# An encoder on one core: tiles moved within a partition, no instruction moved

## The chip, the cores and the metric

The kernel runs on one core of a Trainium2 chip. The metric is the device time of one execution in microseconds. Before the change it is 599.91 us, the median of three runs (599.82 to 600.35).

## What is computed

Two layers, each a mixer and a feed-forward, on 256 tokens of 1,024 numbers, all in float32:

```
for l in range(2):
    h = rms_norm(x, norm1_g[l]);  proj = h @ w_in[l]            # 1024 x 2560
    out_a, out_d, out_c = three kinds of attention on parts of proj (4, 6 and 6 heads of 64)
    mix = concat(rms_norm(out_a), rms_norm(out_d), rms_norm(out_c)) * out_norm_g[l]
    x = x + mix @ w_out[l]                                      # 1024 x 1024
    h = rms_norm(x, norm2_g[l])
    g, u = split(h @ w_gate_up[l], 2)                           # 1024 x 5632
    g = depthwise_conv_of_3(g, conv_w[l]) + conv_b[l]
    x = x + (gelu(g) * u) @ w_down[l]                           # 2816 x 1024
```

## The kernel before

**Products in parts.** A float32 matrix is split into a high part `hi`, rounded to the format `float32r` that TensorE takes, and a low part `lo`, the rest. A product is then a sum of matmuls of parts. Weights come in units of up to 2,048 columns per partition: a DMA on SP's queue brings a unit to a tile `wp_raw` (4 of them), ScalarE casts it to `wp_hi`, VectorE subtracts to get `wp_lo` (2 tiles of each), in pieces of 512 or 1,024 columns (`split`, line 716). Activations are split in the same way: `act_hT` holds the turned, normed input of a layer's half, high and low part side by side (512 numbers for each of 8 blocks of 128 features); `act_mixT_hi` and `act_mixT_lo` the turned attention output; `act_ch` and `act_cl` the gated activations of the feed-forward.

**Kinds of matmul.** A matmul takes 128 columns of one operand as its stationary weights and streams the other operand past them. The names in a row of the profile stand as out<-stream and weights, not always in that order, so here is which is which:

- *Projections* (`mm3` in `projections`, line 942): three matmuls per block, `act_hT` stationary, `wp_hi` or `wp_lo` streamed, 384, 256 or 512 columns wide, into the accumulators `psa_a`.
- *Output projection* (line 966): the same, with `act_mixT_*` stationary, 512 wide. For a few of its units in the second layer, weights that were split earlier are kept in other tiles (`act_qc`, `act_kc`, `act_mixT_*`).
- *Gate and up* (`half_up`, line 1369): the weights are stationary. For each of 8 blocks `large` streams 512 columns of `act_hT` (high and low part) past `wp_hi`, and `little` streams 256 (the high part) past `wp_lo`, into `psw_w`. Mostly eight large ones follow each other, then eight little ones.
- *Down* (`down`, line 1456): `act_ch` or `act_cl` stationary, `wp_hi` or `wp_lo` streamed, 512 wide, into `psa_a`. The last block of columns at the very end is done in halves of 256.

Transposes, scores and the products of probabilities with values are smaller matmuls of other tiles.

**Order.** The kernel records all its operations and then orders them with a planner of its own: costs by engine and shape, and a table `PLACES` that shifts single operations. Every instruction is issued from line 511, so all rows of the profile have that line. The steps of the feed-forward follow the list `FFN` (line 82): gate, down of the step before, up.

**Places in memory.** Each partition's tiles lie one behind the other, in the order in which they are first used. `Slots.place` (line 180) makes a tile as wide as its widest user; the allocator rounds its size up to 32 bytes. So one small tile early on moves all that come after it. In the program before, counted in bytes from the start of a partition, modulo 256:

```
tile                                       before   after the change
act_hT (weights, or the stream)                96       0
wp_hi                                          96       0
wp_lo, projections, output and down            96       0
wp_lo, gate and up                             96     224
act_mixT_hi, act_mixT_lo                      224       0
act_ch, act_cl                                 64       0
act_qc, act_kc, act_qo, act_ko, act_pT, act_z 224       0
const_ident                                   128       0
const_x                                       128       0
const_v (values)                               64       0
```

Inside these tiles the operands of full products begin at multiples of 512 bytes, so the numbers above are those of the operands too.

Of the kernel before, what the change touches and what calls it, by code (L numbers as in the profile page):

```python
# [12 lines left out]
F32R = mybir.dt.float32r  # L13
# [5 lines left out]
P = 128  # L19
S = 256  # L20
NT = S // P
D = 1024
# [14 lines left out]
UNIT = 2048  # L37
BANK = 512
NS2K = 5
NPT = 9  # L40

TURN_ACT = ("d", "dca")
# [4 lines left out]
RAWS, PARTS, AHEAD, CHUNK = 4, 2, 2, 512  # L47
# [34 lines left out]
FFN = [("G", 0), ("U", 0)]  # L82
# [88 lines left out]
class Slots:  # L171
# [7 lines left out]

    def place(self, t):  # L180
        if t.slot not in self.places:
            shape = list(t.shape) if self.dram else [P, BANK if self.psum else self.cols]
            self.places[t.slot] = self.pool.real.tile(
                shape, self.dtype, tag=f"{self.tag}{t.slot}", name=f"{self.pool.name}_{self.tag}{t.slot}", bufs=1
            )
        return self.places[t.slot]
# [83 lines left out]
class Plan:  # L270
# [5 lines left out]
    def pool(self, real, name, bufs, space=bass.MemoryType.SB):  # L276
        return PlanPool(self, real, name, bufs, space)
# [76 lines left out]
    def order(self):  # L354
# [82 lines left out]
        while len(done) < len(ops):  # L437
# [27 lines left out]
            for t in o.tiles:  # L465
                if t.slot is None:
                    s = t.pool
                    s.given += 1
                    place = min(s.free)
                    s.free.remove(place)  # L470
                    t.since, t.slot = taken_at(place[0], ""), place[1]
# [89 lines left out]
def encoder_kernel(  # L561
# [25 lines left out]
    const = pool("const", 1)  # L587
    wp = pool("wp", 3)
    act = pool("act", 2)
    small = pool("small", 4)  # L590
# [12 lines left out]

    gl0 = act.tile([16, P], F32, tag="s2k", name="gl0", bufs=NS2K)
    gl1 = act.tile([32, P], F32, tag="s2k", name="gl1", bufs=NS2K)
    gains = const.tile([P, 3, DEPTH, KD], F32, tag="gains", name="gains")
# [10 lines left out]
        nc.vector.tensor_copy(gains[:, i : i + n].rearrange("p a l k -> p (a l k)"), ps[:, :w])  # L617


    warm = const.tile([P, P], mybir.dt.bfloat16, tag="warm", name="warm")  # L620
    nc.gpsimd.memset(warm, 1.0)
    nc.gpsimd.memset(ident, 0.0)
    nc.gpsimd.affine_select(ident, ident, [[-1, P]], ALU.not_equal, 1.0, base=0, channel_multiplier=1)
# [42 lines left out]
    PER_LAYER = len(views) // DEPTH  # L666
    LAST_OUT = PER_LAYER - len(FFN)
# [48 lines left out]
    def split(i):  # L716
        v = views[i]
        a, b = v.shape[1], v.shape[2]
        n = a * b
        raw = raws[i]  # L720
        if isinstance(raw, list):
            parts.append(raw)
            return
        hi = wp.tile([P, UNIT], F32R, tag="hi", name=f"hi{i}", bufs=PARTS)
        lo = wp.tile([P, UNIT], F32R, tag="lo", name=f"lo{i}", bufs=PARTS)
        h = b if i < 2 else b * max(1, CHUNK // b)
        if i in kept:
            for d, z in zip(kept[i], (hi, lo)):
                nc.gpsimd.dma_start(z[:, :n], d)
        for c in range(0, n if i not in kept else 0, h):  # L730
            e = min(c + h, n)
            nc.scalar.copy(hi[:, c:e], raw[:, c:e])
            nc.vector.tensor_tensor(lo[:, c:e], raw[:, c:e], hi[:, c:e].bitcast(F32), op=ALU.subtract)
        r = lambda z: z[:, :n].rearrange("p (a b) -> p a b", b=b)
        parts.append((r(hi), r(lo)))

    def unit():

        i = taken[0]
        taken[0] += 1  # L740
        with nc.later(SPLIT_LATER):
            while len(raws) < min(i + AHEAD + RAWS - PARTS, len(views)):
                load(len(raws))
            while len(parts) < min(i + AHEAD, len(views)):
                split(len(parts))
        return parts[i]
# [40 lines left out]
    def mean_squares(name):  # L787

        ss = small.tile([P, NT, 2], F32, tag="ssx", name=f"ssx_{name}", bufs=2)
        for h in range(2):  # L790
            for t in range(NT):
                junk = act.tile([P, 512], F32, tag="s2k", name=f"sq_{name}{t}{h}", bufs=NS2K)
                nc.scalar.activation(
# [136 lines left out]
    for l in range(DEPTH):  # L930
# [3 lines left out]
        if l == 0:  # L934
            gains_T(0, 1)
            split(0)
# [78 lines left out]
        def normed(ps, nh, t, name):  # L1015

            w = nh * HD
            sq = act.tile([P, 512], F32, tag="s2k", name=f"sq_{name}", bufs=NS2K)
            ss = small.tile([P, 8], F32, tag="ss", name=f"ss_{name}")
# [80 lines left out]
        class Head:  # L1100
# [4 lines left out]
            def softens(self, sps, whole):  # L1105

                name, bias = self.name, self.bias
                self.p = p = act.tile([P, NT, S], F32, tag="s2k", name=f"p_{name}", bufs=NS2K)
                nm = small.tile([P, NT], F32, tag="nm", name=f"nm_{name}")
                rs = small.tile([P, NT], F32, tag="rs", name=f"rs_{name}")  # L1110

                if bias is not None:
                    sb = act.tile([P, NT, S], F32, tag="s2k", name=f"sb_{name}", bufs=NS2K)
                    for t in range(NT):
# [22 lines left out]
            def turn(self):  # L1137
# [7 lines left out]
                odd = self.h % 2  # L1145
                self.pT = act.tile([P, NT, S], F32, tag="pT", name=f"pT_{name}", bufs=NPT)
                with nc.later(TURN_LATER):
# [436 lines left out]
```

## Time and profile before

| | |
|---|---|
| median of three runs | 599.91 us |
| the profiled execution | 599.53 us |
| its span, first to last instruction | 597.4 us |
| TensorE, busy | 592.0 us, 3,424 matmuls |
| VectorE, busy | 471.0 us |
| ScalarE, busy | 412.7 us |
| GpSimd, busy | 77.1 us |
| granted TensorE clock | 1.000 |
| moved by DMA | 121.37 MB |

How to read the rows: PE is TensorE, PEld its weight load, DVE VectorE, ACT ScalarE, POOL GpSimd. In the list of groups a row has the line, the engine, the operation, the tiles as out<-in without their numbers, the shape and how often it occurs, then the busy time in us, the mean of one in ns, and the engine's idle time before them. In the timeline a row has its start and length in us and how many like instructions follow each other in it (x8). A stretch (`200.00:270.00`) has its length, the busy time and count of PE, PEld, DVE, ACT and POOL, then the granted clock, the DMA engines' busy share and GB/s. A matmul's busy time overlaps with the next one's, since they are pipelined: the distance between starts is what a matmul takes from the span.

### The profile page before, as it was taken

The numbers are of one execution on the slowest core, as the hardware profiler recorded it, in microseconds if no ns is written. First come the engines' busy times: TensorE is split into PE (matmuls) and PEld (weight loads), VectorE is DVE, ScalarE is ACT, GpSimd is POOL, SyncE is SP. The second block draws the span as 40 slices with busy tenths as digits, with TensorE's granted clock in tenths as the row PEclk, the third lists the DMA queues.
The fourth block names the chain that finished last, engine by engine and source line by source line (L and its number), as shares of the span: only waits on it lengthen the run. The fifth ranks groups of instructions, "written<-read, shape, count | busy, mean of one in ns | idle before, by whom it ended". The sixth has DMA issues, their size and how long they took to land.

```text
span 597.4 us, 9676 instructions
## 1 busy us (share of the span) xinstructions
PE 592.0 (99%) x3424; PEld 509.8 (85%) x3424; DVE 471.0 (79%) x983; ACT 412.7 (69%) x1035; POOL 77.1 (13%) x126
## 2 busy tenths in 40 slices
PE   8999999999999999999999999999999999999997
PEld 6999787888888888888899988778888888888886
DVE  5789889878778998698866897768886777668865
ACT  7789987785574677577686998676756656556661
POOL 1723211250000000000032314311000000000000
PEclk9999999999999999999999999999999999999999
DMA  8995315465599699899455727942554664665701
GB/s 281 300 273 163 110 36 159 164 211 189 185 257 360 223 344 306 295 315 332 157 159 156 251 71 247 356 157 90 188 169 161 202 202 137 212 211 183 234 7 71
DMA packets 85072, 121.37 MB, mean 203 GB/s; under 512 B 9864, under 2 KB 69736, under 8 KB 85024
## 3 DMA queue, kind: packets, MB, share of 16 engines
q1 hardware_dynamic: 82752, 112.10, 57.5%
q0 software_dynamic: 1728, 8.39, 4.0%
q8 instruction: 27, 0.44, 0.3%
q10 hardware_dynamic: 544, 0.26, 0.1%
q14 instruction: 21, 0.17, 0.1%
HBM read 110.86 MB, written 9.88 MB: 202 GB/s over the span
## 4 chain that ended last, share of the span: by engine, by line
PE 97%; ACT 1%; DMA 1%; SPq 0%; issue 0%; DVE 0%; ACTq 0%
PE psw_w L511 51%; PE psa_a L511 46%; DMA const_x<-in_x_dram 1%; ACT act_s2k L511 0%; ACT act_hT L511 0%; ACT wp_hi L511 0%; SPq L511 0%; DVE const_x L511 0%; ACTq L511 0%
## 5 line engine op out<-in xcount | busy, mean ns | idle before, releaser
L511 DVE TENSOR_TENSOR wp_lo<-wp_raw,wp_hi 128x512 fp32r<-128x512 f32 (+2 forms) x332 | 234.4, 736 | 42.3 <-ACT wp_hi L511 31.0
L511 ACT CAST wp_hi<-wp_raw 128x512 fp32r<-128x512 f32 (+2 forms) x332 | 203.7, 668 | 22.1 <-PE psa_a L511 11.0
L511 PE MATMUL psw_w<-act_hT,wp_hi 128*128 128x512 f32 x704 | 182.2, 393 | 0.0
L511 PEld LDWEIGHTS psw_w<-act_hT,wp_hi 128*128 128x128 f32 x704 | 128.2, 189 | 23.7
L511 PE MATMUL psa_a<-wp_hi,act_hT 128*128 128x384 f32 (+2 forms) x448 | 112.0, 333 | 0.3 <-ACT wp_hi L511 0.3
L511 PEld LDWEIGHTS psw_w<-act_hT,wp_lo 128*128 128x128 f32 x704 | 99.1, 190 | 7.4
L511 PE MATMUL psw_w<-act_hT,wp_lo 128*128 128x256 f32 x704 | 104.3, 282 | 0.0
L511 PEld LDWEIGHTS psa_a<-wp_hi,act_hT 128*128 128x128 f32 x448 | 77.8, 189 | 3.5 <-DVE act_hT L511 0.5
L511 PE MATMUL psa_a<-wp_lo,act_hT 128*128 128x384 f32 (+2 forms) x224 | 74.5, 335 | 0.0
L511 PE MATMUL psa_a<-wp_lo,act_ch 128*128 128x512 f32 (+1 forms) x176 | 69.3, 394 | 0.0
L511 ACT COPY act_s2k<-psw_w 128x256 f32<-128x256 f32 x88 | 32.2, 370 | 53.0 <-PE psw_w L511 52.5
L511 DVE TENSOR_TENSOR act_s2k<-psw_w,act_s2k 128x256 f32<-128x256 f32 x88 | 36.6, 421 | 39.7 <-ACT act_s2k L511 39.4
L511 PE MATMUL psa_a<-wp_hi,act_cl 128*128 128x512 f32 (+1 forms) x176 | 67.6, 392 | 0.0
L511 PE MATMUL psa_a<-wp_hi,act_ch 128*128 128x512 f32 (+1 forms) x176 | 66.6, 392 | 0.0
L511 PEld LDWEIGHTS psa_a<-wp_lo,act_hT 128*128 128x128 f32 x224 | 42.3, 189 | 1.8 <-DVE wp_lo L511 0.3
L511 PEld LDWEIGHTS psa_a<-wp_hi,act_cl 128*128 128x128 f32 x176 | 33.1, 188 | 7.3
L511 PEld LDWEIGHTS psa_a<-wp_lo,act_ch 128*128 128x128 f32 x176 | 33.1, 188 | 7.1
L511 DVE SCALAR_TENSOR_TENSOR act_s2k<-act_s2k,act_cw,act_s2k 128x255 f32<-128x255 f32 x88 | 37.4, 480 | 1.8 <-ACT act_s2k L511 1.6
L511 PEld LDWEIGHTS psa_a<-wp_hi,act_ch 128*128 128x128 f32 x176 | 32.8, 188 | 6.6
L511 ACT ACTIVATE act_s2k<-act_s2k,act_cw 128x256 f32<-128x256 f32 x44 | 24.1, 595 | 19.9 <-DVE act_s2k L511 19.7
L511 POOL TENSOR_TENSOR small_rstd<-small_ms,const_mh 128x6 f32<-128x6 f32 (+2 forms) x26 | 31.9, 1226 | 15.4 <-DVE small_ms L511 13.8
L511 ACT ACTIVATE act_s2k<-act_s2k 128x512 f32<-128x512 f32 x22 | 13.9, 632 | 26.3 <-DVE act_s2k L511 26.3
(131 smaller groups left out, 705.2 us busy)
## 6 DMA issues: line engine op xcount, KB each, us to landing
wp_raw<-in_w_gate_up_dram SPq DMA_DIRECT2D x44, 1024.0 KB, 5.1
wp_raw<-in_w_down_dram SPq DMA_DIRECT2D x22, 1024.0 KB, 5.1
wp_raw<-in_w_in_dram SPq DMA_DIRECT2D x14, 768.0 KB, 4.6
wp_raw<-in_w_in_dram SPq DMA_DIRECT2D x8, 1024.0 KB, 5.8
wp_raw<-in_w_out_dram SPq DMA_DIRECT2D x8, 768.0 KB, 8.5
dram_khi<-act_mixT_hi SPq DMA_DIRECT2D x4, 768.0 KB, 6.9
dram_klo<-act_mixT_lo SPq DMA_DIRECT2D x4, 768.0 KB, 11.7
wp_lo<-dram_klo POOLq DMA_DIRECT2D x4, 768.0 KB, 6.3
```

The lines of the kernel that those rows point to most:

```text
L511: getattr(o.engine.real, o.method)(*map(real, o.args), **{k: real(v) for k, v in o.kw.items()})
```

## The change

It alters only where tiles begin. Every tile on the chip outside the pool `small` gets a size that is a multiple of 64 elements (256 bytes, for elements of 4 bytes). The tile `warm` of 2-byte elements is made 192 columns wide and used as 128, so that what follows it begins at 0 modulo 256 bytes. The two tiles `wp_lo` are made 64 columns wider; for the units of gate and up the low part is written, and read, 56 columns (224 bytes) further on in them, for all other units at their start.

```
+EVEN, ASIDE = 64, 56
...
-            shape = list(t.shape) if self.dram else [P, BANK if self.psum else self.cols]
+            cols = self.cols if self.pool.name == "small" else -(-self.cols // EVEN) * EVEN
+            shape = list(t.shape) if self.dram else [P, BANK if self.psum else cols]
...
-    warm = const.tile([P, P], mybir.dt.bfloat16, tag="warm", name="warm")
+    warm = const.tile([P, 3 * EVEN], mybir.dt.bfloat16, tag="warm", name="warm")[:, :P]
...
-        lo = wp.tile([P, UNIT], F32R, tag="lo", name=f"lo{i}", bufs=PARTS)
+        lo = wp.tile([P, UNIT + EVEN], F32R, tag="lo", name=f"lo{i}", bufs=PARTS)
+        j = i % PER_LAYER - LAST_OUT
+        lo = lo[:, ASIDE : ASIDE + UNIT] if j >= 0 and FFN[j][0] != "D" else lo[:, :UNIT]
```

On each of the five engines the two programs have the same instructions in the same order (1,958 rows on TensorE, 739 on VectorE, 575 on ScalarE, 114 on GpSimd, 140 on SP); only line numbers and addresses differ.

## The prediction

> **What bounds the kernel now.** I read the page's head, the groups of waits, the busy times by stretch, and the timeline of TensorE, in that order.
>
> ```profile
> span 597.4 us, 9676 instructions
> PE 592.0 (99%) x3424; PEld 509.8 (85%) x3424; DVE 471.0 (79%) x983; ACT 412.7 (69%) x1035; POOL 77.1 (13%) x126
> PE psw_w L511 51%; PE psa_a L511 46%; DMA const_x<-in_x_dram 1%; ACT act_s2k L511 0%; ACT act_hT L511 0%; ACT wp_hi L511 0%; SPq L511 0%; DVE const_x L511 0%; ACTq L511 0%
> ...
> PE psa_a L511 <- POOL const_warm L511: 1.0, 1, 1.0
> PE psw_w L511 <- DMA const_x<-in_x_dram: 0.5, 1, 0.5
> PE psa_a L511 <- ACT wp_hi L511: 0.3, 1, 0.3
> ...
> 200.00:270.00 70.00, 70.00 (x370) 59.95 (x369) 58.16 (x101) 46.16 (x86) 0.00 (x0) 1.00 0.91 317
> 399.00:594.00 195.00, 194.86 (x1038) 166.99 (x1036) 145.66 (x254) 115.08 (x215) 2.98 (x5) 1.00 0.48 161
> ```
>
> TensorE is 97% of the chain that ended last, and all its waits for another engine or a DMA come to 1.8 us, none of them in the two feed-forward stretches shown. There VectorE, the next busiest, works 58.16 of 70 us and 145.66 of 195. So the time is the sum of the spacings between the starts of matmuls. A "busy" mean says nothing of that spacing (393 ns is shown where starts stand 230 ns apart), so everything below is worked from start times in the timeline.
>
> **Two paces.** The change moves no instruction. What it can alter is how fast TensorE reads its two operands: the streamed one, and the weights of the next product, which load meanwhile. Here are three shapes in the projections, where both operands lie at 96 modulo 256 bytes, a difference (weights minus stream) of 0:
>
> ```profile
> 352.91 0.39 PE L511 MATMUL psa_a<-wp_lo,act_hT 128*128 128x512 f32 x1
> 353.13 0.62 PE L511 MATMUL psa_a<-wp_hi,act_hT 128*128 128x512 f32 x2
> 353.59 0.39 PE L511 MATMUL psa_a<-wp_lo,act_hT 128*128 128x512 f32 x1
> 353.81 0.84 PE L511 MATMUL psa_a<-wp_hi,act_hT 128*128 128x512 f32 x3
> 354.49 0.39 PE L511 MATMUL psa_a<-wp_lo,act_hT 128*128 128x512 f32 x1
> 354.72 0.62 PE L511 MATMUL psa_a<-wp_hi,act_hT 128*128 128x512 f32 x2
> ...
> 321.78 0.51 PE L511 MATMUL psa_a<-wp_hi,act_hT 128*128 128x384 f32 x2
> ...
> 325.94 0.34 PE L511 MATMUL psa_a<-wp_lo,act_hT 128*128 128x384 f32 x1
> ...
> 340.74 0.28 PE L511 MATMUL psa_a<-wp_lo,act_hT 128*128 128x256 f32 x1
> ...
> 343.02 0.28 PE L511 MATMUL psa_a<-wp_lo,act_hT 128*128 128x256 f32 x1
> ```
>
> Width 512: 8 spacings in 1.81 us, 226 ns. Width 384: 24 in 4.16 us, 173.3 ns. Width 256: 19 in 2.28 us, 120.0 ns. From 256 to 384 it is 53.3 ns for 128 columns, 0.417 ns each; the 512 follows (226.7). So at difference 0 a settled product costs its columns plus 13.3 ns whatever its width. Now the products of other differences: down-projection (stream at 96, weights at 64, difference -32), the same with half the width at the very end, and the output projection (stream 96, weights 224, difference 128).
>
> ```profile
> 443.14 0.39 PE L511 MATMUL psa_a<-wp_hi,act_ch 128*128 128x512 f32 x1
> ...
> 448.04 0.39 PE L511 MATMUL psa_a<-wp_hi,act_cl 128*128 128x512 f32 x1
> 448.26 1.98 PE L511 MATMUL psw_w<-act_hT,wp_hi 128*128 128x512 f32 x8
> 450.08 1.12 PE L511 MATMUL psw_w<-act_hT,wp_lo 128*128 128x256 f32 x8
> ...
> 591.01 0.28 PE L511 MATMUL psa_a<-wp_hi,act_ch 128*128 128x256 f32 x1
> ...
> 593.46 0.28 PE L511 MATMUL psw_w<-wp_lo,act_ch 128*128 128x256 f32 x1
> ...
> 391.18 0.39 PE L511 MATMUL psa_a<-wp_lo,act_mixT_hi 128*128 128x512 f32 x1
> ...
> 391.87 0.41 PE L511 MATMUL psa_a<-wp_hi,act_mixT_lo 128*128 128x512 f32 x1
> 392.11 0.40 PE L511 MATMUL psa_a<-wp_hi,act_mixT_hi 128*128 128x512 f32 x1
> ...
> 394.20 0.39 PE L511 MATMUL psa_a<-wp_hi,act_mixT_lo 128*128 128x512 f32 x1
> ```
>
> Down: 22 spacings from 443.14 to 448.26, 232.7 ns; the run never comes down to 226.7. Output projection: 13 in 3.02 us, 232.3. Half-width down: 21 in 2.45 us, 116.7 ns, less than the 120.0 of difference 0. Off 0 the surcharge grows with the width: about 20 ns on 213.3, 10 on 106.7. So **difference 0 is better for 512 columns and worse for 256.** Last, the feed-forward's gate and up, both operands at 96:
>
> ```profile
> 440.35 2.00 PE L511 MATMUL psw_w<-act_hT,wp_hi 128*128 128x512 f32 x8
> 442.19 1.11 PE L511 MATMUL psw_w<-act_hT,wp_lo 128*128 128x256 f32 x8
> ```
>
> Eight large ones take 1.84 us (230 ns) when they follow little ones, 1.82 (227.5) after a down run at 448.26: a large run starts at the slow pace and settles after some five products, at a cost of about 8 x 230 - 8 x 226.7 = 27 ns. Eight little ones take 0.95 us, 118.75 ns each.
>
> **The change part by part.** The counts:
>
> ```profile
> L511 PE MATMUL psw_w<-act_hT,wp_hi 128*128 128x512 f32 x704 | 182.2, 393 | 0.0
> L511 PE MATMUL psw_w<-act_hT,wp_lo 128*128 128x256 f32 x704 | 104.3, 282 | 0.0
> L511 PE MATMUL psa_a<-wp_lo,act_ch 128*128 128x512 f32 x172 | 68.2, 397 | 0.0
> L511 PE MATMUL psa_a<-wp_hi,act_mixT_lo 128*128 128x512 f32 x56 | 22.3, 407 | 0.0
> ```
>
> *Down products* (three groups of 172, so 516) go from difference -32 to 0. A run of 22 then costs 22 x 226.7 + 27 = 5.01 us in place of 5.12: 0.11 us per 22, 4.8 ns each, 2.4 us in all. Bounds: 0 (they don't settle) and 516 x 6.0 = 3.1 us (settled throughout).
>
> *Output projection* (three groups of 56, 168) goes from 128 to 0. Its runs are short, cut by transposes and scores, so most of a run is settling time. I take 2 ns each, 0.35 us; bounds 0 and 168 x 5.6 = 0.9 us.
>
> *Little products* (704) get the difference that the half-width down has now: stream at 0, weights at 224, so -32. Of eight in a row, the last streams while weights at 0 load; so 616 gain 118.75 - 116.7 = 2.05 ns: 1.3 us. Bounds 0 and 616 x (120.0 - 116.7) = 2.0 us.
>
> *Large products* (704) keep difference 0, but the last of eight now streams while weights at 224 load. That is 88 products at up to 232.7 - 226.7 = 6 ns; half of it, since one load can disturb only part of a pattern that repeats over several products: a loss of 0.3 us (0 to 0.5). Whether a run settles sooner or later when it follows little products of the new pace, no row tells: 704 x (230 - 226.7) = 2.3 us of gain if always settled, 704 x (232.7 - 230) = 1.9 us of loss if never. I take 0, and both for the range.
>
> *All else*: projections of 384 and 256 keep difference 0 and only move from 96 to 0 together: 0. The casts that write the low parts write 224 bytes further on VectorE, under TensorE, which waits for none of them: 0; were TensorE 4 us faster, VectorE would still have 195 - 145.66 = 49 us to spare in the second stretch and 11.8 of 70 in the first.
>
> Sum: 2.4 + 0.35 + 1.3 - 0.3 = 3.75 us. The profiled execution took 599.53 us (597.4 of span), 0.38 under the median of 599.91; against the median I forecast **596.2 us**, with 594.5 to 598 as its own range.
>
> **The rivals.**
>
> *Deeper settling (about 591.5 us).* A settled stream is not disturbed any more: large 2.3, down 3.1, output 0.9, little 2.0, together 8.3 us. For it: after a down run, large ones hardly need to settle. Against: at difference 0 they do need it after little ones.
>
> *Place counts, not only difference (about 578 us).* If streams at 96 pay for beginning in the middle of some unit of 64 bytes or more, 0 could halve the 13.3 ns for all 704 + 704 + 516 + 384 + 192 + 168 products: 2,668 x 6.7 = 17.9 us on top of the 3.75. Against: 13.3 ns is just 32 columns' time at each of three widths, which leaves no odd piece for a torn unit, and no row has a stream at another place to compare.
> [...]
>
> *Addresses don't matter (599.9).* Two operands with a way of their own each would leave every spacing as it is, and the differences in pace would come from what the matmuls write or from neighbours. Against: 120.0 and 116.7 ns at one width, both into the same accumulators psa, and 226 against 232.7.
> [...]
>
> *Collision at place 0 (about 603 us).* Both operands of a full product now begin at the start of a 256-byte unit, and may meet there on every product instead of falling into the settled pace. The 512 wide ones would then run between the slow pace, 232.7 ns, and the worst single spacing of the rows above, 240 ns (391.87 to 392.11). At 234 the large pay 704 x 4 = 2.8 us, the down ones 516 x 1.3 = 0.7, the output ones 168 x 1.7 = 0.3; 384 columns at the slow pace's surcharge (19.4 ns on 512, so 14.6 on 384) pay 1.3 x 384 = 0.5; the little ones, off 0, still save 1.3: 3.0 us slower. It decides from the point where no large run settles: at 232.7 it is 1.9 + 0.5 - 1.3 = 1.1 us. For it: no row has a product at place 0. Against: the three projection shapes settle with operands at many distances of 512 bytes and more from each other, so 96 alone is hardly what lets them.
>
> **How the numbers follow.** Forecast 0.52, deeper settling 0.14, place counts 0.07, no effect 0.13, collision 0.14. What this kernel's measurement tells from no change is about 0.2%, 1.2 us. Faster by more: 0.52 + 0.14 + 0.07 = 0.73, less 0.01 for a forecast that comes out too small to tell: 0.72. Same: 0.14. Slower: 0.14. The range runs from 589, a little under the deeper settling, to 601.5, which takes in the mild end of the collision; it leaves out the place rival and the collision's worse half.
>
> **What would show it.** Down runs with starts 226.7 ns apart after the first few show the first term right; 232 or more, wrong. Little ones at 0.93 us or less for eight show the third. Large runs at 1.84 for eight show that the start of the pattern is as now, 1.81 the second rival's way, 1.87 the collision. A 384 wide product at 166.7 instead of 173.3 would show that place counts. TensorE waits above 3 us in the waits table would show a new bound, which I don't expect.

## The result

The changed kernel takes 595.85 us (median of four runs, 595.50 to 596.06) against 600.04 us before (599.82 to 600.35): a ratio of 0.9929, with a 95% interval of 0.9912 to 0.9946, so 4.2 us less. Its profiled execution took 595.66 us. First the page of the profile after, and TensorE's waits:

```profile
span 593.6 us, 9680 instructions
PE 588.1 (99%) x3424; PEld 508.0 (86%) x3424; DVE 470.9 (79%) x983; ACT 412.6 (70%) x1035; POOL 77.2 (13%) x126
...
PE psa_a L513 <- POOL const_warm L513: 1.0, 1, 1.0
PE psw_w L513 <- DMA const_x<-in_x_dram: 0.5, 1, 0.5
PE psa_a L513 <- ACT wp_hi L513: 0.4, 1, 0.4
```

The waits are the same three, 1.9 us where they were 1.8; all of VectorE's and ScalarE's work is as before. The 3.9 us of TensorE's busy time are gone from the spacing of its matmuls. Then the timeline of TensorE after, at the places that the prediction showed of before: gate and up, then a down run.

```profile
435.29 2.01 PE L513 MATMUL psw_w<-act_hT,wp_hi 128*128 128x512 f32 x8
437.14 1.10 PE L513 MATMUL psw_w<-act_hT,wp_lo 128*128 128x256 f32 x8
438.07 2.01 PE L513 MATMUL psw_w<-act_hT,wp_hi 128*128 128x512 f32 x8
439.92 1.10 PE L513 MATMUL psw_w<-act_hT,wp_lo 128*128 128x256 f32 x8
440.85 0.40 PE L513 MATMUL psa_a<-wp_hi,act_ch 128*128 128x512 f32 x1
...
442.24 0.39 PE L513 MATMUL psa_a<-wp_hi,act_ch 128*128 128x512 f32 x1
...
445.64 0.39 PE L513 MATMUL psa_a<-wp_hi,act_cl 128*128 128x512 f32 x1
445.87 1.98 PE L513 MATMUL psw_w<-act_hT,wp_hi 128*128 128x512 f32 x8
447.69 1.10 PE L513 MATMUL psw_w<-act_hT,wp_lo 128*128 128x256 f32 x8
...
587.05 0.28 PE L513 MATMUL psa_a<-wp_hi,act_ch 128*128 128x256 f32 x1
...
589.56 0.28 PE L513 MATMUL psw_w<-wp_lo,act_ch 128*128 128x256 f32 x1
```

The down run of 22 takes 445.87 - 440.85 = 5.02 us (it was 5.12): the first six spacings 231.7 ns, the other sixteen 226.9. Eight little ones take 0.93 us (0.95), eight large ones 1.85 after little ones (1.84) and 1.82 after the down run, as before. And the half-width products at the very end went the other way: 21 spacings in 2.51 us, 119.5 ns in place of 116.7.

From the starts in the timeline, all spacings summed by kind of the matmul that begins them, in us (waits are in them; "other" is transposes, scores and values). The columns behind the second are runs that come below; "again" is a second profiled execution of the changed kernel.

```
                before  after   again place96  aside0  both   alone  aside52  narrow  pair
large           162.16 162.40  163.41  162.41  162.03  164.67 162.62  161.75  161.75 161.07
little           83.67  82.22   82.34   82.21   83.68   82.57  82.29   82.11   82.12  82.71
down            120.40 117.81  117.83  117.85  117.89  118.05 120.42  117.66  117.65 118.19
down, halves      2.68   2.75    2.75    2.75    2.75    2.75   2.68    2.75    2.75   2.75
output           47.24  47.01   46.96   47.04   46.99   46.99  47.27   46.99   47.07  47.05
projections 384  69.26  69.25   68.97   69.27   69.13   68.52  68.67   69.12   68.65  68.61
projections 256  24.21  24.23   24.24   24.25   24.25   24.23  24.72   24.22   23.85  23.87
projections 512  23.41  23.38   23.38   23.37   23.38   23.40  23.67   23.36   23.55  23.55
other            59.57  59.65   61.20   60.21   59.47   60.36  60.60   59.68   59.78  60.53
span            597.4  593.6   595.9   594.2   594.4   596.4  597.8   592.5   592.0  593.2
of it, first 53  11.1   11.0    12.1    11.7    10.8    11.1   10.5    11.0    10.6   11.3
from the 54th   586.4  582.5   583.8   582.6   583.6   585.3  587.3   581.4   581.4  581.9
```

The last two rows part the span at the start of the 54th matmul. The stretch before it, with its waits for the first inputs, differs by up to 1.1 us between two executions of the same program ("after" and "again"), so small differences are read from the last row. "Again" has besides one wait of 0.8 us for VectorE at 180 us, which costs its large and little products 1.1 us; without that the two agree within 0.2 us in the last row.

### The profile page after: what moved, and what is told of

It reads as the page before. It is cut to its first block, busy times and chain, and to the rows that moved or that the text cites. A ratio compares the mean times of both kernels' runs of the same rounds, so it can differ in the third digit from the quotient of the medians.

```text
span 593.6 us, 9680 instructions
## 1 busy us (share of the span) xinstructions
PE 588.1 (99%) x3424; PEld 508.0 (86%) x3424; DVE 470.9 (79%) x983; ACT 412.6 (70%) x1035; POOL 77.2 (13%) x126
## 4 chain that ended last, share of the span: by engine, by line
PE 97%; ACT 1%; DMA 1%; SPq 0%; issue 0%; DVE 0%; ACTq 0%
PE psw_w L513 51%; PE psa_a L513 46%; DMA const_x<-in_x_dram 1%; ACT act_s2k L513 0%; ACT act_hT L513 0%; ACT wp_hi L513 0%; SPq L513 0%; DVE const_x L513 0%; ACTq L513 0%
## 5 line engine op out<-in xcount | busy, mean ns | idle before, releaser
L513 PE MATMUL psw_w<-act_hT,wp_lo 128*128 128x256 f32 x704 | 102.8, 279 | 0.0
```

Of the source, the lines that this page charges most:

```text
L513: getattr(o.engine.real, o.method)(*map(real, o.args), **{k: real(v) for k, v in o.kw.items()})
```

## The experiments

The theory is the prediction's: the difference between the place of the weights that load and the place of the stream, modulo 256 bytes, sets a pace; 512 columns settle at 226.7 ns where it is 0. Its rivals are that the place itself counts, that a settled pace is a matter of which product it is, or that addresses don't matter at all.

**The disputed pace by itself.** A kernel of nothing but matmuls, with the loop

```
for width in (512, 384, 256):
    for shift in range(-128, 129, 16):
        some("s", RUN, width, 0, shift)      # RUN = 24; the stream at 0, the weights `shift` bytes on
...
for width in (512, 256):
    for at in (16, 32, 64, 96, 128):
        for shift in (0, -32):
            some(f"at{at}", RUN, width, at, shift)
```

> This kernel leaves out the whole encoder: it only runs 24 matmuls of one width after each other, 512, 384 or 256 columns, for each difference between the place of the weights and the place of the stream (modulo 256 bytes) from -128 to 128 bytes in steps of 16, and then for differences 0 and -32 with the stream at 16, 32, 64, 96 and 128 bytes. Theory (the difference decides): at difference 0 the last of 24 stand 226.7, 173.3 and 120.0 ns apart for the three widths, at -32 about 233.3, 175 and 116.7; the result for a difference is the same at every place of the stream. Rival (the place decides): at difference 0 the spacing changes with the place of the stream, by more than 2 ns. Rival (only what the encoder does around the matmuls matters): all differences within 1 ns of each other. Not known: which differences other than 0 have a settled pace, and where 256 columns run fastest.

Its timeline has one row for each run of 24; the name of the output tells place, width and difference (m is minus, p plus), and the next row's start, less this one's, over 24 is the spacing:

```profile
42.05 5.76 PE L44 MATMUL sw512xm32B<-m,w 128*128 128x512 f32 x24
47.65 5.62 PE L44 MATMUL sw512xm16B<-m,w 128*128 128x512 f32 x24
53.12 5.60 PE L44 MATMUL sw512xp0B<-m,w 128*128 128x512 f32 x24
58.55 5.61 PE L44 MATMUL sw512xp16B<-m,w 128*128 128x512 f32 x24
64.00 5.75 PE L44 MATMUL sw512xp32B<-m,w 128*128 128x512 f32 x24
...
191.51 2.96 PE L44 MATMUL sw256xm32B<-m,w 128*128 128x256 f32 x24
194.31 3.04 PE L44 MATMUL sw256xm16B<-m,w 128*128 128x256 f32 x24
197.18 3.04 PE L44 MATMUL sw256xp0B<-m,w 128*128 128x256 f32 x24
200.05 3.01 PE L44 MATMUL sw256xp16B<-m,w 128*128 128x256 f32 x24
...
222.71 5.71 PE L44 MATMUL at16w512xp0B<-m,w 128*128 128x512 f32 x24
228.26 5.74 PE L44 MATMUL at16w512xm32B<-m,w 128*128 128x512 f32 x24
233.84 5.61 PE L44 MATMUL at32w512xp0B<-m,w 128*128 128x512 f32 x24
239.28 5.76 PE L44 MATMUL at32w512xm32B<-m,w 128*128 128x512 f32 x24
...
255.96 5.64 PE L44 MATMUL at96w512xp0B<-m,w 128*128 128x512 f32 x24
261.43 5.76 PE L44 MATMUL at96w512xm32B<-m,w 128*128 128x512 f32 x24
267.03 5.64 PE L44 MATMUL at128w512xp0B<-m,w 128*128 128x512 f32 x24
```

At 512 columns difference 0 takes 5.43 us (226 ns), -32 takes 5.60 (233); at 256 columns it is 2.87 (119.6) and 2.80 (116.7). Both signs are as in the encoder, with nothing of the encoder left, so the rival that addresses don't matter falls. At the places 32 and 96 difference 0 takes 5.44 and 5.47, -32 5.60 and 5.60: the same as at 0, but for the settling. At place 16 difference 0 takes 5.55 (231 ns), and its spacings don't fall to 226.7: at the one place tried that is not a multiple of 32 bytes the place counts after all, in one run of 24. In the encoder the tiles in the table of places begin at multiples of 32, before and after. All differences, the mean of the last twelve spacings inside each run in ns:

```
bytes -128  -112   -96   -80   -64   -48   -32   -16     0    16    32    48    64    80    96   112   128
512  231.7 226.8 233.3 230.0 233.3 233.3 233.3 226.8 226.8 226.7 233.4 233.3 233.3 232.1 234.2 233.4 233.4
384  175.8 177.2 176.7 173.4 173.3 175.6 176.8 173.4 173.3 173.3 173.3 173.3 173.3 176.2 173.3 173.3 176.4
256  118.9 120.1 120.0 118.1 117.8 116.8 116.7 120.0 120.0 118.6 118.6 117.8 113.4 118.8 117.3 120.5 120.0
```

So 0 is not alone: in runs of 24, -112, -16 and 16 settle too at 512 columns. And of the differences for 256 only 64 is faster than -32. The columns -128 and 128 are the same place modulo 256 bytes, and they differ by 0.6 to 1.7 ns, so less than that tells nothing here. The last run of the kernel, at 512 columns and difference 256, stands at 226.7 ns, as difference 0 does.

**Same differences, every place 96.** `warm` is 240 columns wide (`3 * EVEN + 48`) and not rounded up, so that every tile begins 96 bytes further.

> The changed kernel with every tile 96 bytes further, so all differences are those of the changed kernel, and the places of projections, gate and up those of the kernel before. Theory (the difference decides): 595.9 us, within 0.4 of the changed kernel; down 226.7 ns apart once settled, little ones at 116.5. Rival (place 0 gives the gain): 598 to 600 us, down back at 232.7.

596.27 us (595.94 to 596.76), ratio to before 0.9937 (0.9921 to 0.9954). In the table above down has 117.85 us and the little ones 82.21, where the change has 117.81 and 82.22. The 0.6 us more of its span lie in the first 53 matmuls; from the 54th on it takes 582.6 us, and the change 582.5. Place 0 gives nothing that 96 doesn't; with it falls the rival of a collision there.

**The 56 columns taken back.**

```
-EVEN, ASIDE = 64, 56
+EVEN, ASIDE = 64, 0
```

> The changed kernel without the 56 columns: the low parts of gate and up at 0 like all else. Theory: the little products go back to 118.8 ns, 704 x 2.0 = 1.4 us, so 597.3 us; down stays at 226.7 settled. Rival (the little products' place does nothing): 595.9 us. If the large ones settle sooner after little ones of difference 0, up to 0.5 us less than 597.3.

596.77 us (596.35 to 597.08), ratio 0.9944 (0.9929 to 0.9959). The little ones go back to 83.68 us, 1.46 more. But the large ones drop from 162.40 to 162.03, so the 56 columns are worth 0.9 us by the medians and 1.1 by the last row of the table, not 1.4. Up to 0.5 less had been allowed for, though for another reason: that the large ones would settle sooner. The spacings of the 22 runs of eight large ones that stand between little ones, first to eighth, in ns:

```
before   233.4 235.4 228.3 232.1 230.7 226.7 226.8 226.6
after    233.0 235.3 228.8 231.8 230.1 227.3 227.1 234.5
aside0   233.5 235.3 228.4 232.3 230.6 226.6 226.6 226.8
```

They don't settle sooner: the first five differ by 0.5 ns at most. The loss sits in the eighth, which streams while the first little one's weights at 224 load (in the run that starts at 435.29 us after, the eighth and that load both start at 436.91, the little one itself at 437.14).

**The large ones at -32 too.**

```
...
+        hi, lo = (z[:, ASIDE : ASIDE + UNIT] if j >= 0 and FFN[j][0] != "D" else z[:, :UNIT] for z in (hi, lo))
```

> The changed kernel with the high parts of gate and up 56 columns further as well, so that the large products have the difference -32 too. Theory (the difference sets the pace, whatever the product is for): the large ones never settle, 233.3 ns against 229.8 now, 704 x 3.5 = 2.5 us, so 598.3 us; the little ones stay at 116.8, down at 226.7 settled. Rival (the slow pace belonged to the down products): 595.9 us.

598.51 us (598.30 to 598.97). In its timeline eight large ones now take 1.87 us, 233.8 ns each, and all 704 take 164.67 us, 2.3 more:

```profile
436.75 2.03 PE L513 MATMUL psw_w<-act_hT,wp_hi 128*128 128x512 f32 x8
438.62 1.10 PE L513 MATMUL psw_w<-act_hT,wp_lo 128*128 128x256 f32 x8
```

They have taken over the pace that down had (233.3 ns before), and down keeps the settled one (118.05 us). So it is the difference and not the product.

**The 56 columns alone**, on the kernel before.

> The kernel before, with the low parts of gate and up 56 columns further and nothing else (all else at its old place). Theory (the parts add up): little products at 116.8 in place of 118.8, 1.4 us; large ones between 229.4 and 229.8, at most 0.3 us lost; so 598.7 us. Rival (the place of the low parts helps only with the rest of the change): 599.9 us.

599.36 us; its ten runs lie between 598.27 and 600.19, ratio 0.9990 (0.9980 to 1.0000). The terms are there: little 82.29 (1.38 less), large 162.62 (0.46 more, where at most 0.3 was expected), down 120.42. But the profiled execution, at 599.89, spends 1.2 us more in the two layers' attention parts, and shows two waits that the kernel before doesn't have:

```profile
PE psw_w L512 <- ACT act_s2k L512: 0.5, 2, 0.3
PE psa_a L512 <- DMA wp_hi<-dram_khi: 0.3, 1, 0.3
```

The terms alone would give 598.9 us. Four of the ten runs lie at 598.3 to 598.6 and five at 599.5 or more, and what makes the two groups is open. By the theory the places of other tiles are no reason: by the program's addresses all of them stay where they were modulo 256 bytes. The time as a whole neither confirms nor refutes that the parts add up; the sums by kind do.

**Turns of large and little.** A kernel of nothing but eight large ones at difference 0 and eight little ones at another, three times each:

```
for shift in range(-128, 129, 16):
    for i in range(3):
        some(f"big{i}_", 8, 512, 0, 0)
        some(f"small{i}_", 8, 256, 0, shift)
```

> This kernel leaves out the whole encoder: it runs eight matmuls of 512 columns at difference 0, then eight of 256 columns at another difference, three times for each such difference from -128 to 128 bytes in steps of 16. Theory (a large run settles from wherever the little run left off): at -32 eight large ones take about 1.84 us and eight little ones 0.93, at 0 1.84 and 0.95; some difference may leave the large ones settled from the start, 1.815 us. Rival (each large run starts anew): the eight large ones take the same at every difference, within 0.01 us.

```profile
55.31 1.09 PE L44 MATMUL small_w256xm48B<-m,w 128*128 128x256 f32 x8
56.24 1.99 PE L44 MATMUL big_w512xp0B<-m,w 128*128 128x512 f32 x8
58.07 1.09 PE L44 MATMUL small_w256xm48B<-m,w 128*128 128x256 f32 x8
...
63.62 1.10 PE L44 MATMUL small_w256xm32B<-m,w 128*128 128x256 f32 x8
64.55 2.01 PE L44 MATMUL big_w512xp0B<-m,w 128*128 128x512 f32 x8
66.40 1.10 PE L44 MATMUL small_w256xm32B<-m,w 128*128 128x256 f32 x8
```

After little ones at -48 the large take 58.07 - 56.24 = 1.83 us, after -32 1.85; a pair of eights takes 2.76 us with -48, 2.78 with -32 (the change) and 2.79 with 0. So a large run does go on from where the little run left it, and no difference from -64 to 128 leaves it at the settled 1.81 us in all three turns: the least is 1.83, 1.82 and 1.82, after little ones at 80. A second kernel of this kind, in steps of 8 bytes from -72 to 0, with single large and little ones by turns and runs of 24 behind them, had the same order of these:

> This kernel leaves out the whole encoder. Turns of eight large products at difference 0 and eight little ones at -72 to 0 bytes in steps of 8, three times each; then for -48, -32 and 0 one large and one little by turns, eight little ones, and a run of 24 large ones. Theory (a run starts from where the last one left off): -48 is best at 2.76 us for 8 and 8, -32 2.78, 0 2.79, -16 2.77 as before; the run of 24 takes 24 x 226.7 = 5.44 us plus 0.007 to 0.03 us. Rival (chance of that one run): other numbers for the same differences, by more than 0.01 us.

-48 took 2.76 us again, -32 2.78, -16 2.77 and 0 2.79; -72, -64, -56, -40, -24 and -8 lay between 2.76 and 2.81. Its runs of 24 after little ones of -48, -32 and 0 took 5.467, 5.456 and 5.459 us, 15 to 26 ns over 24 x 226.7, which is what settling costs a run of this length. Single large products between single little ones took 227 to 241 ns and never settled.

**52 columns.**

```
-EVEN, ASIDE = 64, 56
+EVEN, ASIDE = 64, 52
```

> The changed kernel with 52 columns in place of 56 (difference -48 in place of -32). From the turns alone: eight large and eight little ones in 2.76 us in place of 2.78, 0.017 us for each of 88 such pairs, 1.5 us less: 594.4 us. If the encoder's other turns (single products, gate and up by turns, down between them) decide how the large ones begin: 595.9 us.

594.51 us (594.26 to 595.84), ratio 0.9915 (0.9900 to 0.9929). Large 161.75 us, 0.65 less than with 56 columns; little 82.11. In the timeline:

```profile
434.76 1.99 PE L513 MATMUL psw_w<-act_hT,wp_hi 128*128 128x512 f32 x8
436.59 1.09 PE L513 MATMUL psw_w<-act_hT,wp_lo 128*128 128x256 f32 x8
437.52 1.99 PE L513 MATMUL psw_w<-act_hT,wp_hi 128*128 128x512 f32 x8
```

1.83 us for eight large, as in the turns. The median is 1.3 us lower, but the kernel before was 0.25 us faster in these rounds too; the profiled span is 1.1 us shorter, and 0.9 of that is in large, little and down. That the time came out as expected (594.4) is in part luck: 1.5 us was to come from 88 pairs of eights, but in the encoder only 22 runs of exactly eight large ones stand between little ones, and the large ones gave 0.65.

**Narrow projections.** On top of the 52 columns: the 192 projection products of 256 columns stream weights; with high and low parts 8 columns further they have difference -32 too.

```
...
+        if b == 2 * P and j < 0:
+            hi, lo = hi[:, 8 : 8 + UNIT], lo[:, 8 : 8 + UNIT]
...
```

> 52 columns for the low parts of gate and up, and high and low weights of the projections of 256 columns 8 columns (32 bytes) further, so that these 192 products stream at 32 past weights at 0, difference -32. Theory: they go from 119.5 to 116.7 ns, 192 x 2.8 = 0.5 us, so 594.0 us where 52 columns alone gave 594.5. Rival (these runs are cut too often by transposes to have a pace): 594.5 us.

> The changed kernel again, on the chip and in the rounds of the kernel with 52 columns and narrow products: 595.9 us, 1.9 above that by the theory (1.4 from the 52 columns, 0.5 from the narrow ones).

594.17 us (593.99 to 594.40), ratio to before 0.9904 (0.9889 to 0.9919); beside it in the same rounds the changed kernel took 596.14 (595.51 to 598.02), 0.9941 (0.9927 to 0.9956). This version beats both kernels; of the 2.0 us over the changed one, 1.1 are in the last row of the table against "after", and the rest is within what the start and a single wait do ("again", the slowest of those five runs, has both). The narrow products went from 24.22 to 23.85 us, 0.37 less where 0.5 was expected, but the projections of 512 columns rose by 0.19 and the output projection by 0.08. From the 54th matmul on it takes 581.39 us and the 52 columns alone 581.45: the narrow products gain 0.06 us in all, so the 0.34 us between the medians is not theirs.

**Other differences for the large ones.** Turns as before, with the large at -112, -16 and 16:

> This kernel leaves out the whole encoder. Turns of eight large and eight little products as before, now with the large ones at difference -112, -16 or 16, the others that settle, and the little ones at -128 to 112 in steps of 16. Theory (a run starts from where the last one left off, so pairs of differences count): most pairs between 2.76 and 2.80 us for 8 and 8, some pair below 2.76; never below 8 x 226.7 + 8 x 113.4 = 2.72. Rival (0 for the large ones is special): all pairs above 2.77 us.

Most pairs took 2.77 to 2.83 us. The only one below 2.76 in all three turns has the large at -16, the little at -64:

```profile
179.91 1.97 PE L44 MATMUL big_w512xm16B<-m,w 128*128 128x512 f32 x8
181.72 1.10 PE L44 MATMUL small_w256xm64B<-m,w 128*128 128x256 f32 x8
182.66 1.98 PE L44 MATMUL big_w512xm16B<-m,w 128*128 128x512 f32 x8
```

1.81 us for eight large: here they are settled from the first. At -112 and at 16, which settled in runs of 24, most eights took 1.86 to 1.87 us, the unsettled pace, and a few 1.82. The pair in the encoder, on top of the version above:

```
-EVEN, ASIDE = 64, 52
+EVEN, ASIDE, HIGH_ASIDE = 64, 48, 60
...
+        if j >= 0 and FFN[j][0] != "D":
+            hi, lo = hi[:, HIGH_ASIDE : HIGH_ASIDE + UNIT], lo[:, ASIDE : ASIDE + UNIT]
```

> The version with 52 columns and narrow products, but in gate and up the high parts 60 columns further (difference -16) and the low parts 48 (difference -64): the pair that was fastest in the turns, 2.753 us for 8 and 8 with the large ones at 226.6 from the first on, against 2.760 for the pair 0 and -48. Theory of the turns alone: 88 x 0.007 = 0.6 us less, 593.6 us, large 160.5 us in all, little 82.8. Rival (in the encoder the turns with down runs, and singles, decide): large between 161.7 and 163, so 594.2 to 596.

594.89 us (594.41 to 595.29), ratio 0.9913 (0.9900 to 0.9927): no better than the version above, and from the 54th matmul on 0.47 us slower. The 22 runs of eight between little ones do what the turns did, 227.5 to 226.2 ns from first to eighth, 13.5 ns less for a run. But that is 0.3 us, and large falls by 0.68 us in all (161.07). Little rises by 0.59 as the turns said (116.6 to 117.5 each), and down by 0.54, which now begins after a stream of another difference. "Other" has 0.75 more, nearly all of it in the first 53 matmuls, where the unchanged program differed as much from itself.

## Why the prediction was right

The forecast was 596.2 us, the measured time 595.85, and the gain came by the steps forecast. By the table of sums, against the working:

- *Down products*, 2.4 us: 120.40 to 117.81, 2.6 us. The products stood 233.3 ns apart before, on the mean of all 516, and 228.3 after, where 232.7 and 227.9 were worked out from one run of 22. That run took 5.02 us where 5.01 was worked out; runs of 23 and 24 need only some 17 ns to settle, and runs of up to six hardly do (230 ns and more). (4.8 ns for 516 products make 2.5 us, not 2.4.)
- *Output projection*, 0.35 us: 0.23.
- *Little products*, 1.3 us: 1.45, which is 2.06 ns for each of all 704; the working had given the last of a run nothing. The row that carried this, the half-width down at the end, proved itself the other way round as well: with difference 0 it slowed from 116.7 to 119.5 ns. That was left out of "all else" as 0; it cost 0.07 us.
- *Large products*, a loss of 0.3 us: 0.24. That the size is right is luck. The working took 88 runs of eight and 3 ns for the last of each, half of 6 by the author's estimate that one load disturbs only part of the pattern (the slow down run of before repeats about 230, 235, 233 and 235 ns); but only 33 runs are of exactly eight, and the eighth pays nearly 8 ns. The 22 of them between little ones lose that; the 11 behind a down run get it back, since they are settled from their first product now (10 ns less in the first seven).
- *All else*, 0: projections within 0.03 us, "other" 0.08 more.

The sum is 2.6 + 0.23 + 1.45 - 0.24 - 0.07 - 0.04 = 3.9 us, and the span fell by 3.9. The medians differ by 0.3 us more than that, which is within their scatter. The one thing for which no row was there, how a large run begins after little ones of the new pace, was taken as no change with 2.3 and 1.9 us to either side. It came out as none for 56 columns (the first five of a run within 0.6 ns), which was luck too: the run with 52 columns gives 0.65 us.

Of the rivals, the place (578 us) falls with the result itself, since the projections of 384 columns kept their 69.25 us; it and the collision at place 0 (603 us) fall with the kernel at 96. That addresses don't matter falls with the streams alone and with the large ones at -32: TensorE's pace depends here on how its own two operands lie to each other (512 columns: 226.7 ns at difference 0 and 233.3 at -32 in the streams, 233.8 for the large ones at -32). Deeper settling didn't happen: down still settles over its first products (231.7 ns for six, then 226.9), and large runs after little ones as before (233.0 ns for the first, 227.3 for the sixth); 1.81 us for eight, which the prediction puts to its second rival, would have been the sign of this first one. That 96 is as good as 0 the kernel at 96 shows (582.6 us from the 54th matmul on, against 582.5); but in the run of streams at place 16 difference 0 didn't settle (231 ns), while it did at 0, 32, 64, 96 and 128 (5.43 to 5.48 us for 24, against 5.60 at -32).

What stays open is why a difference has its pace. One difference can have two: the little ones at 64 ran at 113.4 ns in the run of streams and at 117.7 in the first turns. And in the last kernel of turns, three runs of eight at -64 between large ones at -112 took 0.91, 0.95 and 0.91 us, so the state in which a run begins belongs to it.

## What to carry to other kernels

Where TensorE is the bound and each matmul loads new weights, as here (busy for 99% of the span, 3,424 loads for 3,424 matmuls), look at the distances between starts of like matmuls in the timeline, not at the mean of one: two paces for one shape (here 226.7 and 233.3 ns at 512 columns) can come from where the operands lie. Here tile sizes that are multiples of 256 bytes, with the weights of short streams set off on purpose, gave 0.7%, and with a better offset for the short streams 0.85%, without a single instruction moved. Measure such offsets in a kernel of streams and turns first, one run of 0.3 ms for dozens of them, but check the best in the kernel itself: the pair that won the turns by 7 ns did not win there.

## What was not expected of the hardware

- The surcharge of a settled matmul is 13.3 ns whatever its width (226.7, 173.3 and 120.0 ns for 512, 384 and 256 columns at difference 0), while at -32 it grows with the width (233.3 and 116.7 ns for 512 and 256).
- Several differences settle at 512 columns in runs of 24: -112, -16, 0 and 16 bytes. In runs of eight between little ones -112 and 16 mostly didn't (1.86 to 1.87 us for eight, against 1.81 settled).
- For 256 columns the differences 64 and -64 ran at about 113.5 ns in some runs, 6.5 below the pace of difference 0, and at 117.7 or more in others, it seems by the state in which the run began.
- Both operands at place 16 cost 231 ns at difference 0, in the one run of it, where multiples of 32 cost 226.7.
